# A hybrid encoder step on one core: one band output product for both parts of the probabilities, and four edits beside it

## The chip, the cores and the metric

The kernel is one launch on one core of a Trainium2 chip. The metric is the device time of the launch in microseconds (us). The engines are TensorE (PE, matmuls; PEld is its weight loading), VectorE (DVE), ScalarE (ACT), GpSimd (POOL) and SyncE (SP), which here issues every DMA.

## The reference

One layer of a streaming encoder over 2048 prompt rows and 32 sample rows of width 1024. What matters for the change is the band attention of eight heads of 64 dims, in which each chunk of 64 rows sees itself and the eight chunks before it, the merge, and the MLP with its gate:

```python
def band_core(q, k, v, bias, mask):
    s = jnp.einsum('bqhd,bkhd->bhqk', q, k).astype(jnp.float32) * (HEAD_DIM ** -0.5) + bias[None]
    s = jnp.where(mask, s, NEG)
    p = jax.nn.softmax(s, axis=-1)
    return jnp.einsum('bhqk,bkhd->bqhd', p.astype(v.dtype), v)

def merge(oa, ob, subln_g, out_norm_b, w_out, lam_init):
    ...
    return jnp.concatenate([oa.reshape(B, T, WIDTH_A), ob], axis=-1) @ w_out

def ffn_ple(h, p, g_mlp, w_up, w_down, w_ple_gate, w_ple_proj):
    c = rmsnorm(h, g_mlp)
    h = h + jnp.square(jax.nn.relu(c @ w_up)) @ w_down
    return h + jax.nn.sigmoid(h @ w_ple_gate) * (p @ w_ple_proj)
```

All inputs are 32-bit. Before these, one projection makes queries, keys and values of a differential attention (group A, four heads) and of the band attention (group B); y is normalized at the end, and new keys and values are outputs too.

## The kernel before

**Numbers in two parts.** A 32-bit number is split (`split`, L177) into a high part, rounded to the matmul's format, and a low part, the rest. A product is three matmuls, high by high, high by low, low by high (`mm3`, L211; its lines L215, L216, L217 stand in the profile for every product made that way, told apart by the name of the output: qps and vps for the projections, ops for the output projection, ups and dps for the MLP's up and down products, gps and pps for the gate). The split's copy runs on ScalarE (L180) or VectorE (L182), its subtraction on GpSimd (L165, L175, cut into pieces of 256 columns) or VectorE (L186).

**Stages.** Tokens are in four blocks of 512 (the last with the 32 sample rows, 544). The program, `run`, goes through: norm and values of blocks 0 and 1; projections and group A attention of the first half (to about 515 us); band attention `attn_b` for four groups of query blocks, among projections, output projection and the first MLP chunks (515 to 1216); group A attention of the second half with the MLP of blocks 0 and 1 (to 2110); gate and final norm of block 1; output projections of blocks 2 and 3, `outproj`, with the loading of the second's input, `oload`, woven in, one unit (`OW` = 1) per step (2160 to 2270); gate of block 0 with `cparts(2)`, the operands of block 2's MLP (to 2327); `mlp7(2)`; gate of block 2 with `cparts(3)`; `mlp7(3)`; gate and final norm of block 3.

**What sets the order.** The code is written as generators that `weave` steps alternately. The framework then schedules with its own timeline model, keeping each engine's program order where priorities say so; so instructions of `attn_b` stand among those of the stages written around it. Every buffer belongs to a tag of a pool with a number of copies, and a tile waits for the last user of the copy that it takes. Every load and store (`dma`, L156) is issued by SP, in order: one that waits holds all behind it.

**Band attention.** `attn_b` loads, per head and query group, keys (kbt), queries and values. `attn_b_pair` takes 256 queries, two tiles of 128 with up to five key tiles each. For each tile: scores in one or two banks, two matmuls each (sb, L802); bias and maximum (L805); exponentials (L810) and the division (L812); transposes of the probabilities (tpb, L817); their high part on ScalarE (pHb, L826) and low part on VectorE (pLb, L827). Behind both tiles stands the output product (ob, L842): the value tile (vbt), which holds 64 high and 64 low columns, is the weight; the high and the low probabilities are two matmuls into the same 256 columns (or 128, for a key tile that only one query tile sees). Rows 0 to 63 of ob are then the high values' part and 64 to 127 the low values' part, which L846 and L847 add.

**Values.** `vtile` makes one 128-row tile of values (vps), scales it (vraw, L421) and splits it into vhl: the copy on VectorE, the subtraction on GpSimd.

**mlp7.** 16 chunks of 256 hidden columns. A chunk's up product uses seven block products in place of eight: from the weight's four quarters a11, a12, a21, a22 it makes a11, a12 and five sums s2, s1, s3, s4, a22, each split into pieces (`piece`). The first product needs a11, the second a12, the third s2. The chunk's down products (dps) are added to h (L1124), which is 2 MB and loaded by `hload` before. ReLU and square make u, split into uh and ul (L1138). Down products of a chunk are stepped among the up products of the next one.

Of the kernel before, what the change touches and what calls it, by code (L numbers as in the profile page):

```python
# [12 lines left out]
F32 = mybir.dt.float32  # L13
# [129 lines left out]
class Kern:  # L143
# [261 lines left out]
    def vtile(self, b, i, grp, c, u, acts, sg, mm):  # L405
# [18 lines left out]
        self.split(hl[:n, :, 0], hl[:n, :, 1], r3[:n], "dve", "pool")  # L424
# [165 lines left out]
    def attn_a_pair(self, g, j, kt, ba, pool, ps_s, ps_t, ps_o):  # L590
# [88 lines left out]
        o = ps_o.tile([P, 256], F32, tag="o", name="o")  # L679
# [48 lines left out]
        ss = ps_o.tile([P, 256], F32, tag="o", name="ss")[:, :nq]  # L728
# [6 lines left out]
    def attn_b(self, js, pool, ps_s, ps_t, ps_o):  # L735
# [3 lines left out]
        ke = KC if last else 256 * (js[-1] + 1)  # L739
        for h in range(8):  # L740
# [21 lines left out]
            for x, j in enumerate(js):  # L762
                nq = 256 if j < 8 else SS
                self.attn_b_pair(
                    h, j if j < 8 else None, kt, v, kb, bb, qs[x], tt[:, 256 * x : 256 * x + nq], pool, ps_s, ps_t, ps_o
                )
# [3 lines left out]
    def attn_b_pair(self, h, j, kt, v, kb, bb, q, t1, pool, ps_s, ps_t, ps_o):  # L770
# [7 lines left out]
        pH = pool.tile([P, 6, 256], F32R, tag="pH", bufs=2, name="pHb")  # L778
        pL = pool.tile([P, 6, 256], F32R, tag="pL", bufs=2, name="pLb")
        spans = []  # L780
        for qi, t in enumerate(tiles):
# [14 lines left out]
            e = pool.tile([P, 640], F32, tag="e", bufs=4, name="eb")[:nr, :n]  # L796
            st = pool.tile([P, 5], F32, tag="st", bufs=4, name="stb")[:nr]
            for i in range(nb):
                s = ps_s.tile([P, 512], F32, tag="s", name="sb")[:nr, :w]
                for hl in range(2):  # L800
                    c = k0 - kb + w * i
                    nc.tensor.matmul(  # L802
                        s, q[:, hl, P * qi : P * qi + nr], kt[:, c : c + w], start=hl == 0, stop=hl == 1
                    )
                nc.vector.tensor_tensor_reduce(  # L805
                    e[:, w * i : w * i + w], s, bb[:nr, b0 + w * i : b0 + w * i + w], 1.0, -3e38,
                    ALU.add, ALU.max, st[:, 3 + i : 4 + i],
                )
            nc.vector.tensor_reduce(st[:, 0:1], st[:, 3 : 3 + nb], axis=AX.X, op=ALU.max, negate=True)
            nc.scalar.activation(e, e, AF.Exp, bias=st[:, 0:1], accum_out=st[:, 1:2])  # L810
            nc.vector.reciprocal(st[:, 2:3], st[:, 1:2])
            nc.scalar.activation(e, e, AF.Copy, scale=st[:, 2:3])  # L812
            for x0 in range(0, len(kts), 4):
                ch = kts[x0 : x0 + 4]
                tp = ps_t.tile([P, 4, P], F32, tag="tp", name="tpb")
                for x, (i, kn) in enumerate(ch):
                    nc.tensor.transpose(  # L817
                        tp[:kn, x, :nr], e[:, P * (x0 + x) : P * (x0 + x) + kn], self.ident[:nr, :nr]
                    )
                groups = [(0, len(ch), P)] if not samp else [(0, 1, P), (1, 1, SS)]  # L820
                for a0, na, kn in groups:
                    sl = ch[0][0] - kfirst + a0
                    h_ = pH[:kn, sl : sl + na, P * qi : P * qi + nr]
                    l_ = pL[:kn, sl : sl + na, P * qi : P * qi + nr]
                    s_ = tp[:kn, a0 : a0 + na, :nr]
                    nc.scalar.activation(h_, s_, AF.Copy)  # L826
                    nc.vector.tensor_tensor(l_, s_, h_.bitcast(F32), op=ALU.subtract)  # L827
        o = ps_o.tile([P, 256], F32, tag="o", name="ob")
        order = []
# [9 lines left out]
        for x, (i, kn, qa, qb) in enumerate(order):  # L839
            vt = v[:kn, (SP - kb) // P + i] if samp else v[:kn, i - kb // P]  # L840
            for y, pt in enumerate((pH, pL)):
                nc.tensor.matmul(  # L842
                    o[:, qa:qb], vt, pt[:kn, i - kfirst, qa:qb],
                    start=x == 0 and y == 0, stop=x == len(order) - 1 and y == 1,
                )
        nc.scalar.activation(t1, o[64:128, :nq], AF.Copy)  # L846
        nc.vector.tensor_tensor(t1, o[0:64, :nq], t1, op=ALU.add)  # L847
# [248 lines left out]
    def mlp7(self, b, h, ops, wk, up, mm, md):  # L1096
# [49 lines left out]
        prev = iter(())  # L1146
        for ch in range(DFF // (2 * P)):
# [9 lines left out]
            w = {}  # L1157
            for x in ("a11", "a12", "s2", "s1", "s3", "s4", "a22"):
                w[x] = self.piece([4, P])
# [7 lines left out]
            for x, t, e in (("s2", s2, "dve"), ("s1", a11, "pool"), ("s3", a21, "dve"), ("s4", a12, "pool"), ("a22", a22, "dve")):  # L1167
                self.split(*w[x], t, "act", e)
            us = []
# [155 lines left out]
    def run(self):  # L1325
        tc, nc, a = self.tc, self.nc, self.a
        with ExitStack() as top:
# [24 lines left out]
            with ExitStack() as x:  # L1352
# [7 lines left out]
                def first():  # L1360
                    self.consts(cp)
# [129 lines left out]
            hh = opened(top, "hh", 2, side="right")  # L1491
# [17 lines left out]
            for _ in range(2):  # L1509
                next(m)  # L1510
# [7 lines left out]
            for _ in range(2):  # L1518
                next(m)
# [52 lines left out]
```

## Time and profile before

| | us |
|---|---|
| time, median of 3 runs | 3192.19 (3191.18 to 3198.04) |
| the profiled execution's own time | 3198.91 |
| its span | 3197.1 |
| TensorE, band attention's window | 515 to 1216 |
| mlp7(2): first up product | 2327.13 |

A row of a timeline gives start, duration, engine, line, operation, tiles, shape and count. A row of waits says which engine stood idle before which group, what it waited for, how long in total, how many times, and the longest. A row of groups gives shape and count, busy time and mean ns of one, and the idle time before them. A matmul's duration runs past the start of the next.

### The profile page before, as it was taken

How to read it: one execution, taken by the hardware profiler on the slowest of the kernel's cores; microseconds unless marked ns; L12 is line 12 of the kernel's file. 1: busy time of each engine (PE TensorE's matmuls, PEld its weight loads, DVE VectorE, ACT ScalarE, POOL GpSimd, SP SyncE). 2: the span in 40 equal slices, each digit the busy share in tenths (PEclk: the TensorE clock that was granted, in tenths of full speed). 3: DMA queues.
4: the chain of work that ended last, by engine and by line, in shares of the span. 5: the costliest groups of instructions: out<-in, count | busy, mean ns of one | idle time of the engine just before them, and what ended most of it. 6: DMA issues, size and time to landing. Idle time of an engine off the chain costs nothing.

```text
span 3197.1 us, 53415 instructions
## 1 busy us (share of the span) xinstructions
PE 3033.6 (95%) x18265; PEld 2684.4 (84%) x18265; DVE 1843.7 (58%) x4448; ACT 1884.9 (59%) x4166; POOL 1890.6 (59%) x2572
## 2 busy tenths in 40 slices
PE   8999898899999998999999999998999999899998
PEld 7787787899987787877788888777888888899998
DVE  5147774444464554766756665435577665776663
ACT  5257775766675765666666666444555555554445
POOL 4357455343335544565655555577887778867674
PEclk9999998999999999999999999999999999999999
DMA  8788757886788746555564543537524334233231
GB/s 274 237 244 232 210 182 230 245 228 201 204 238 238 212 120 148 153 154 151 158 184 123 142 126 104 156 109 225 172 87 147 106 100 128 92 100 107 93 114 55
DMA packets 512504, 521.61 MB, mean 163 GB/s; under 512 B 37948, under 2 KB 393600, under 8 KB 512232
## 3 DMA queue, kind: packets, MB, share of 16 engines
q1 hardware_dynamic: 512232, 518.19, 55.4%
q8 instruction: 145, 2.38, 0.3%
q14 instruction: 127, 1.04, 0.1%
HBM read 412.08 MB, written 109.95 MB: 163 GB/s over the span
## 4 chain that ended last, share of the span: by engine, by line
PE 65%; DVE 11%; DMA 10%; ACT 5%; POOL 4%; issue 4%; SPq 1%; DVEq 0%; POOLq 0%; ACTq 0%
PE dps L215 6%; PE dps L217 6%; PE dps L216 6%; PE ups L215 6%; PE ups L216 5%; PE ups L217 5%; PE qps L215 3%; PE qps L216 3%; PE qps L217 3%; PE s L632 3%; DMA oraw<-oT 2%; PE ob L842 2%; PE sb L802 1%; DMA wr<-w_up 1%; PE tpb L817 1%
## 5 line engine op out<-in xcount | busy, mean ns | idle before, releaser
L175 POOL TENSOR_TENSOR wl<-wr,wh 128x256 fp32r<-128x256 f32 x648 | 479.5, 773 | 344.4 <-ACT wh L180 311.5
L180 ACT ACTIVATE piece<-wr 128x512 fp32r<-128x512 f32 x412 | 252.7, 626 | 288.5 <-PE ups L216 139.2
L175 POOL TENSOR_TENSOR piece<-wr,piece 128x256 fp32r<-128x256 f32 x416 | 338.7, 840 | 103.9 <-ACT piece L180 85.2
L180 ACT ACTIVATE wh<-wr 128x1024 fp32r<-128x1024 f32 x228 | 240.7, 1056 | 180.3 <-PE qps L216 46.6
L165 POOL TENSOR_TENSOR wl<-wr,wh 128x256 fp32r<-128x256 f32 x264 | 196.3, 775 | 171.3 <-ACT wh L180 171.1
L215 PE MATMUL ups<-cs,piece 128*128 128x256 f32 (+1 forms) x896 | 257.0, 287 | 10.2 <-ACT piece L180 7.6
L217 PE MATMUL ups<-cs,piece 128*128 128x256 f32 (+1 forms) x896 | 257.1, 287 | 5.6 <-POOL piece L175 5.6
L216 PE MATMUL ups<-cs,piece 128*128 128x256 f32 (+1 forms) x896 | 256.1, 286 | 0.5 <-DVE cs L186 0.5
L216 PE MATMUL dps<-ul,piece 128*128 128x272 f32 (+1 forms) x768 | 247.7, 324 | 1.6 <-DVE ul L186 1.6
L217 PE MATMUL dps<-uh,piece 128*128 128x272 f32 (+1 forms) x768 | 247.5, 324 | 1.3 <-POOL piece L165 1.3
L215 PE MATMUL dps<-uh,piece 128*128 128x272 f32 (+1 forms) x768 | 246.4, 324 | 1.5 <-DVE h L1124 0.8
L165 POOL TENSOR_TENSOR piece<-wr,piece 128x256 fp32r<-128x256 f32 x280 | 224.3, 833 | 25.7 <-ACT piece L180 24.3
L1124 DVE TENSOR_TENSOR h<-h,dps 128x272 f32<-128x272 f32 (+1 forms) x384 | 190.6, 514 | 81.4 <-PE dps L217 80.4
L215 PE MATMUL qps<-aH,wh 128*128 128x512 f32 (+1 forms) x640 | 230.8, 361 | 6.9 <-DVE ql L475 4.8
L1083 DVE TENSOR_TENSOR h<-h,dps 128x512 f32<-128x512 f32 x256 | 174.2, 682 | 96.3 <-PE dps L217 94.7
L217 PE MATMUL qps<-aH,wl 128*128 128x512 f32 (+1 forms) x640 | 229.2, 358 | 0.0
L216 PE MATMUL qps<-aL,wh 128*128 128x512 f32 (+1 forms) x640 | 228.9, 358 | 0.0
L215 PE MATMUL dps<-uh,wh 128*128 128x512 f32 x512 | 211.3, 413 | 13.7 <-DVE h L1083 8.6
L632 PE MATMUL s<-ka,q 128*128 128x512 f32 (+3 forms) x768 | 187.6, 343 | 25.4 <-ACT e L646 17.5
L215 PE MATMUL ups<-cH,wh 128*128 128x512 f32 x512 | 203.6, 398 | 1.6 <-DVE h L1083 0.9
L638 DVE TENSOR_REDUCE nm<-s 128x1 f32<-128x512 f32 (+3 forms) x256 | 147.2, 587 | 98.9 <-PE s L632 97.9
L217 PE MATMUL dps<-uh,wl 128*128 128x512 f32 x512 | 204.0, 398 | 0.0
(298 smaller groups left out, 9793.3 us busy)
## 6 DMA issues: line engine op xcount, KB each, us to landing
wr<-w_up SPq DMA_DIRECT2D x128, 512.0 KB, 4.0
wr<-w_down SPq DMA_DIRECT2D x128, 512.0 KB, 3.7
wr<-w_in SPq DMA_DIRECT2D x74, 512.0 KB, 5.1
q<-qS SPq DMA_DIRECT2D x128, 256.0 KB, 5.4
v<-vSa SPq DMA_DIRECT2D x64, 512.0 KB, 4.3
ka<-kS SPq DMA_DIRECT2D x32, 512.0 KB, 9.0
wr<-w_out SPq DMA_DIRECT2D x32, 512.0 KB, 5.2
wr<-w_ple_gate SPq DMA_DIRECT2D x32, 512.0 KB, 3.9
```

Source lines behind the costliest of these rows:

```text
L165: nc.gpsimd.tensor_tensor(out[:, sl], a[:, sl], b[:, sl], op=op)
L175: nc.gpsimd.tensor_tensor(out[:, sl], a[:, sl], b[:, sl], op=op)
L180: nc.scalar.activation(hi, raw, AF.Copy)
L215: nc.tensor.matmul(ps, lh, rh, start=start and i == 0, stop=False)
L216: nc.tensor.matmul(ps, lh, rl, start=False, stop=False)
L217: nc.tensor.matmul(ps, ll, rh, start=False, stop=stop and i == n - 1)
L632: nc.tensor.matmul(s, q[:, m, hl, P * qi : P * qi + nr], kt[:, m, k0 - kb : k0 - kb + n], start=hl == 0, stop=hl == 1)
L638: nc.vector.tensor_reduce(nmx, s, axis=AX.X, op=ALU.max, negate=True)
L802: nc.tensor.matmul(s, q[:, hl, P * qi : P * qi + nr], kt[:, c : c + w], start=hl == 0, stop=hl == 1)
L842: nc.tensor.matmul(o[:, qa:qb], vt, pt[:kn, i - kfirst, qa:qb], start=x == 0 and y == 0, stop=x == len(order) - 1 and y == 1,)
L1083: nc.vector.tensor_tensor(hv, hv, ps, op=ALU.add)
L1124: nc.vector.tensor_tensor(hv, hv, ps, op=ALU.add)
```

## The change

Five edits.

1. The output product of the band moves to `attn_b_out`: high and low probabilities lie side by side in one tile pb, [128, 6, 2, 256], and each key tile is one matmul over both, 512 columns (or two times 128). The two halves of ob are 256 columns each, of a full bank; a further addition on VectorE adds the low probabilities' part. The product of the low values with the low probabilities, which was in the sum, is left out of it.
2. In the band, `step` and `late` write a tile's transposes (and, with the pair's second tile, the output product and a head's store) behind the next tile's scores.
3. `oload(3)` is stepped by two units for each step of `outproj(2)`.
4. `mlp7` makes chunk 0's first four pieces (a11, a12, s2, s1) in its first step, which `along` puts into the gate before it, once `cparts` is done. They lie in a buffer of the size of h ("lead"), taken from the pool hh, which becomes two pools of one buffer. The rest of chunk 0's pieces are made in the next step. h of the block (`box`) takes the lead's buffer, so its load waits for the last product that reads the lead.
5. `vtile`'s subtraction goes from GpSimd to VectorE.

```diff
@@ vtile
-        self.split(hl[:n, :, 0], hl[:n, :, 1], r3[:n], "dve", "pool")
+        self.split(hl[:n, :, 0], hl[:n, :, 1], r3[:n], "dve", "dve")
@@ attn_b
+        late = []
+
+        def step(first):
+            ins = first()
+            if late:
+                with self.tc.issue_after(ins):
+                    late.pop(0)()
+
...
-            self.dma(self.oT[64 * m : 64 * m + 64, gi, t0 : t0 + n], tt[:, :n])
...
+            late.append(self.then(late.pop(), lambda m=m, gi=gi, tt=tt, t0=t0, n=n: self.dma(
+                self.oT[64 * m : 64 * m + 64, gi, t0 : t0 + n], tt[:, :n]
+            )))
+        late.pop(0)()
@@ attn_b_pair
-        pH = pool.tile([P, 6, 256], F32R, tag="pH", bufs=2, name="pHb")
-        pL = pool.tile([P, 6, 256], F32R, tag="pL", bufs=2, name="pLb")
...
+            def first(qi=qi, nr=nr, k0=k0, n=n, b0=b0, nb=nb, w=w, held=held):
...
+                return ins.ins
+
+            def second(qi=qi, nr=nr, kts=kts, held=held, end=t is tiles[-1]):
+                if qi == 0:
+                    px.append(pool.tile([P, 6, 2, 256], F32R, tag="p", bufs=2, name="pb"))
+                p = px[0]
...
+                        h_, l_ = (p[:kn, sl : sl + na, i, P * qi : P * qi + nr] for i in range(2))
...
+                if end:
+                    self.attn_b_out(samp, nq, spans, kfirst, kb, v, px[0], t1, ps_o)
+
+            step(first)
+            late.append(second)
+
+    def attn_b_out(self, samp, nq, spans, kfirst, kb, v, p, t1, ps_o):
+        nc = self.nc
+        o = ps_o.tile([P, 512], F32, tag="o", name="ob").rearrange("p (i c) -> p i c", i=2)
...
-            for y, pt in enumerate((pH, pL)):
-                nc.tensor.matmul(
-                    o[:, qa:qb], vt, pt[:kn, i - kfirst, qa:qb],
-                    start=x == 0 and y == 0, stop=x == len(order) - 1 and y == 1,
-                )
-        nc.scalar.activation(t1, o[64:128, :nq], AF.Copy)
-        nc.vector.tensor_tensor(t1, o[0:64, :nq], t1, op=ALU.add)
+            nc.tensor.matmul(
+                o[:, :, qa:qb], vt, p[:kn, i - kfirst, :, qa:qb], start=x == 0, stop=x == len(order) - 1
+            )
+        nc.scalar.activation(t1, o[64:128, 0, :nq], AF.Copy)
+        nc.vector.tensor_tensor(t1, o[0:64, 0, :nq], t1, op=ALU.add)
+        nc.vector.tensor_tensor(t1, o[0:64, 1, :nq], t1, op=ALU.add)
@@ mlp7
+    def along(self, c, m):
+        for _ in c:
+            yield
+        yield
+        next(m)
+        yield
...
+        def weights(ch, w, piece):
...
+            self.split(*w["s2"], s2, "act", "dve")
+            self.split(*w["s1"], a11, "act", "pool")
+            yield
+            for x in ("s3", "s4", "a22"):
+                w[x] = self.piece([4, P])
+            for x, t, e in (("s3", a21, "dve"), ("s4", a12, "pool"), ("a22", a22, "dve")):
                 self.split(*w[x], t, "act", e)
+
+        w = {}
+        lead = hh.tile([P, 8, BLK], F32R, tag="h", name="lead").rearrange("p k c -> p (k c)")
+        leads = iter(lead[:, 512 * i : 512 * i + 512].rearrange("p (k c) -> p k c", c=P) for i in range(8))
+        g = weights(0, w, lambda shape: [next(leads), next(leads)])
+        next(g)
+        yield
+        drain(g)
+        h = hh.tile([P, 8, BLK], F32, tag="h", name="h")
+        self.dma(h[:, :, :n], self.hS[:, :, 512 * b : 512 * b + n])
+        box.append(h)
@@ run
-            hh = opened(top, "hh", 2, side="right")
+            hh = [opened(top, f"hh{i}", 1, side="right") for i in range(2)]
...
-                weave(self.outproj(2, wk, oa[2], md, acc[2]), self.oload(3, wk, act, oa), 1, 0, OW)
+                weave(self.outproj(2, wk, oa[2], md, acc[2]), self.oload(3, wk, act, oa), 1, 0, 2)
...
-            weave(g, self.cparts(2, wk, cs, ops, r2), 1)
+            c = self.cparts(2, wk, cs, ops, r2)
+            next(c)
+            box = []
+            m = self.mlp7(2, hh[1], box, ops[2], wk, up, mm, md)
+            weave(g, self.along(c, m), 1)
             f = self.final(0, h, up, fk, mm)
-            h = hload(hh, BLK, 2)
-            m = self.mlp7(2, h, ops[2], wk, up, mm, md)
             for _ in range(2):
                 next(m)
+            h = box[0]
             weave(m, f, 1)
```

The same is done for block 3, whose lead lies in hh[0].

On PE, at a full pair of the band, before (ob is the output product, tpb the transposes):

```order
L842 MATMUL ob<-pLb,vbt 128x256
L842 MATMUL ob<-pHb,vbt 128x256
L842 MATMUL ob<-pLb,vbt 128x256
L842 MATMUL ob<-pHb,vbt 128x256
L842 MATMUL ob<-pLb,vbt 128x256
L842 MATMUL ob<-pHb,vbt 128x256
L842 MATMUL ob<-pLb,vbt 128x256
L842 MATMUL ob<-pHb,vbt 128x128
L842 MATMUL ob<-pLb,vbt 128x128
L842 MATMUL ob<-pHb,vbt 128x128
L842 MATMUL ob<-pLb,vbt 128x128
L817 MATMUL tpb<-ident,eb 128x128 x5
```

and after, with the scores (sb) of the tile ahead and pieces of a value projection (vps):

```order
L824 MATMUL sb<-kbt,q 128x320 x2
L217 MATMUL vps<-wh,aL 128x256
L215 MATMUL vps<-wh,aH 128x256
L216 MATMUL vps<-wl,aH 128x256
L876 MATMUL ob<-pb,vbt 128x512 x4
L876 MATMUL ob<-pb,vbt 128x2x128 x2
L846 MATMUL tpb<-ident,eb 128x128 x5
```

Twelve matmuls (the first stands a few rows ahead, before a projection's) became six, and the next tile's scores and a projection stand before them.

On SP, whose rows are the DMAs in their order (h of block 2, and wr for every raw weight), at the end of the second output projection, before:

```order
L156 DMA hd_25587<-xT_76 128x544
L156 DMA hd_25670<-xT_76 128x544
L156 DMA h_26788<-hS_82 128x8x512
L156 DMA wr_26205<-w_ple_proj 128x2x512
L156 DMA hS_82<-hd_25587 128x544
L156 DMA hS_82<-hd_25670 128x544
```

and at mlp7(2)'s beginning, before, where each pair of w_up rows is a chunk:

```order
L156 DMA wr_26952<-w_up 128x4x256
L156 DMA wr_27041<-w_down 128x2x512
L156 DMA wr_27135<-w_down 128x2x512
L156 DMA wr_27198<-w_up 128x4x256
L156 DMA wr_27200<-w_up 128x4x256
```

The same beginning after; the four w_up rows are chunk 1's and chunk 2's two halves (chunk 0's stand far ahead, in the gate):

```order
L156 DMA wr_26594<-w_up 128x4x256
L156 DMA wr_26685<-w_down 128x2x512
L156 DMA wr_26596<-w_up 128x4x256
L156 DMA wr_26779<-w_down 128x2x512
L156 DMA wr_26842<-w_up 128x4x256
L156 DMA h_26473<-hS_82 128x8x512
L156 DMA wr_26844<-w_up 128x4x256
L156 DMA wr_26933<-w_down 128x2x512
L156 DMA wr_27027<-w_down 128x2x512
```

The load of h, 2 MB, went from ahead of the gate to between the two halves of chunk 2.

On DVE, in chunk 1 of mlp7(2), before (u2, u3, r0, r1 are block products, ul the low part of a chunk's u, s2 and wr the weight sums of chunk 2, h the sum with the down products):

```order
L1135 TENSOR_TENSOR r1_26836<-u3_26896,ups_26931 128x256
L1163 TENSOR_TENSOR wr_27198<-wr_27198 128x4x128
L186 TENSOR_TENSOR ul_26832<-r0_26835,uh_26831 128x512
L1135 TENSOR_TENSOR r0_26995<-t1_26997,ups_27012 128x256
L1164 TENSOR_TENSOR s2_27222<-wr_27200,wr_27198 128x512
L1135 TENSOR_TENSOR u2_27026<-t1_26997,ups_27027 128x256
L1135 TENSOR_TENSOR u3_27084<-u2_27026,ups_27085 128x256
L1165 TENSOR_TENSOR wr_27198<-s2_27222,wr_27198 128x4x128
L1124 TENSOR_TENSOR h_26788<-h_26788,dps_27053 128x512
```

and after:

```order
L1176 TENSOR_TENSOR r0_26479<-u2_26510,ups_26557 128x256
L1176 TENSOR_TENSOR r0_26639<-t1_26641,ups_26656 128x256
L1176 TENSOR_TENSOR u2_26670<-t1_26641,ups_26671 128x256
L1204 TENSOR_TENSOR s2_26860<-wr_26844,wr_26842 128x512
L186 TENSOR_TENSOR ul_26476<-r0_26479,uh_26475 128x512
L186 TENSOR_TENSOR piece_26851<-s2_26860,piece_26850 128x512
L1205 TENSOR_TENSOR wr_26842<-s2_26860,wr_26842 128x4x128
L1176 TENSOR_TENSOR u3_26728<-u2_26670,ups_26729 128x256
L1176 TENSOR_TENSOR r0_26639<-u2_26670,ups_26761 128x256
L1165 TENSOR_TENSOR h_26473<-h_26473,dps_26697 128x512
```

Chunk 0's ul stood ahead of the operation that takes both halves of chunk 2 (L1164, now L1204) and now stands behind it.

More of the change, by code (lines that the diff above doesn't have):

```diff
@@ L809, in attn_b_pair @@
[L809 to L827, printed above, removed]
@@ L828, in attn_b_pair @@
-        o = ps_o.tile([P, 256], F32, tag="o", name="ob")
-        order = []
+            held = []
+            def first(qi=qi, nr=nr, k0=k0, n=n, b0=b0, nb=nb, w=w, held=held):
+                e = pool.tile([P, 640], F32, tag="e", bufs=4, name="eb")[:nr, :n]
+                st = pool.tile([P, 5], F32, tag="st", bufs=4, name="stb")[:nr]
+                held.append(e)
+                for i in range(nb):
+                    s = ps_s.tile([P, 512], F32, tag="s", name="sb")[:nr, :w]
+                    for hl in range(2):
+                        c = k0 - kb + w * i
+                        ins = nc.tensor.matmul(
+                            s, q[:, hl, P * qi : P * qi + nr], kt[:, c : c + w], start=hl == 0, stop=hl == 1
+                        )
+                    nc.vector.tensor_tensor_reduce(
+                        e[:, w * i : w * i + w], s, bb[:nr, b0 + w * i : b0 + w * i + w], 1.0, -3e38,
+                        ALU.add, ALU.max, st[:, 3 + i : 4 + i],
+                    )
+                nc.vector.tensor_reduce(st[:, 0:1], st[:, 3 : 3 + nb], axis=AX.X, op=ALU.max, negate=True)
+                nc.scalar.activation(e, e, AF.Exp, bias=st[:, 0:1], accum_out=st[:, 1:2])
+                nc.vector.reciprocal(st[:, 2:3], st[:, 1:2])
+                nc.scalar.activation(e, e, AF.Copy, scale=st[:, 2:3])
+                return ins.ins
@@ new lines, in second @@
+            def second(qi=qi, nr=nr, kts=kts, held=held, end=t is tiles[-1]):
+                if qi == 0:
+                    px.append(pool.tile([P, 6, 2, 256], F32R, tag="p", bufs=2, name="pb"))
+                p = px[0]
+                e = held[0]
+                for x0 in range(0, len(kts), 4):
+                    ch = kts[x0 : x0 + 4]
+                    tp = ps_t.tile([P, 4, P], F32, tag="tp", name="tpb")
+                    for x, (i, kn) in enumerate(ch):
+                        nc.tensor.transpose(
+                            tp[:kn, x, :nr], e[:, P * (x0 + x) : P * (x0 + x) + kn], self.ident[:nr, :nr]
+                        )
+                    groups = [(0, len(ch), P)] if not samp else [(0, 1, P), (1, 1, SS)]
+                    for a0, na, kn in groups:
+                        sl = ch[0][0] - kfirst + a0
+                        h_, l_ = (p[:kn, sl : sl + na, i, P * qi : P * qi + nr] for i in range(2))
+                        s_ = tp[:kn, a0 : a0 + na, :nr]
+                        nc.scalar.activation(h_, s_, AF.Copy)
+                        nc.vector.tensor_tensor(l_, s_, h_.bitcast(F32), op=ALU.subtract)
+                if end:
+                    self.attn_b_out(samp, nq, spans, kfirst, kb, v, px[0], t1, ps_o)
@@ L1513, in run @@
             next(g)
[L1514 removed]
+            c = self.cparts(3, wk, cs, ops, r3)
+            next(c)
+            box = []
+            m = self.mlp7(3, hh[0], box, ops[3], wk, up, mm, md)
+            weave(g, self.along(c, m), 1)
             f = self.final(2, h, up, fk, mm)
[L1516 to L1517 removed]
             for _ in range(2):
                 next(m)
+            h = box[0]
             weave(m, f, 1)
```

49 lines of the change are left out of this document (22 added, 27 removed).

## The prediction

> **What bounds the kernel now.** I read the page first, for which engine carries the end, then the stretch that the largest edit touches, then the waits of the places that the other edits aim at. The page:
>
> ```profile
> span 3197.1 us, 53415 instructions
> PE 3033.6 (95%) x18265; PEld 2684.4 (84%) x18265; DVE 1843.7 (58%) x4448; ACT 1884.9 (59%) x4166; POOL 1890.6 (59%) x2572
> PE 65%; DVE 11%; DMA 10%; ACT 5%; POOL 4%; issue 4%; SPq 1%; DVEq 0%; POOLq 0%; ACTq 0%
> ```
>
> TensorE (PE) is busy 95% of the span and has 65% of the chain that ended last; every other engine is under 60%. So time comes off where PE's instructions get fewer or shorter, or where PE stands waiting; other engines' work counts only when PE waits for it. The window from 515 to 1216 us holds the band attention, interleaved with projections, output products and the first MLP chunks (columns: window, length, busy time of PE, PEld, DVE, ACT, POOL, granted clock, DMA share, GB/s):
>
> ```profile
> 515.00:1216.00 701.00, 670.45 (x4359) 603.37 (x4358) 350.16 (x1233) 465.98 (x982) 305.93 (x472) 0.99 0.73 208
> ```
>
> PE is busy 670 of 701 us there, VectorE (DVE) 350. What PE is spared in this window shortens it almost one for one, and VectorE has half its time free.
>
> **A, the band's output product.** A matmul's duration overlaps its neighbours', so its price is the distance from its start to the next one's. PE's timeline gives it, 512 columns first, then 256, then 128:
>
> ```profile
> 839.82 0.40 PE L217 MATMUL qps<-aH,wl 128*128 128x512 f32 x1
> 840.52 0.40 PE L217 MATMUL qps<-aH,wl 128*128 128x512 f32 x1
> 861.46 0.28 PE L842 MATMUL ob<-pLb,vbt 128*128 128x256 f32 x1
> 862.17 0.28 PE L842 MATMUL ob<-pLb,vbt 128*128 128x256 f32 x1
> 862.28 0.22 PE L842 MATMUL ob<-pHb,vbt 128*128 128x128 f32 x1
> 862.34 0.28 PE L842 MATMUL ob<-pLb,vbt 128*128 128x128 f32 x1
> 862.68 0.51 PE L817 MATMUL tpb<-ident,eb 128*128 128x128 f32 x3
> ```
>
> The first two are three matmuls apart: 0.70/3 = 0.233 us for 512 columns. The next two are six apart: 0.71/6 = 0.118 for 256. From 862.34 to the transposes at 862.68 are three: 0.34/3 = 0.113 for 128, hardly less than for 256, so a matmul of 128 columns is held up by something other than its columns. The counts:
>
> ```profile
> L842 PE MATMUL ob<-pHb,vbt 128*128 128x256 f32 x224 | 59.7, 287 | 1.0 <-ACT pHb L826 1.0
> L842 PE MATMUL ob<-pLb,vbt 128*128 128x128 f32 x112 | 29.6, 277 | 0.0
> ```
>
> With as many of the other part, that is 448 of 256 columns and 224 of 128. The change makes 224 of 512 and 112 of two times 128, which I price as one of 256. Of the 224, 192 are in 48 full query pairs (8 heads, j = 2 to 7). Such a pair had 8 of 256 and 4 of 128; the eleven of one pair that the timeline shows in a row take 862.68 - 861.46 = 1.22, and the twelfth 0.118: 1.34. After, 4 × 0.233 + 2 × 0.118 = 1.17. That is 0.17 × 48 = 8.2 us less. The two short pairs of each head lose one or three double matmuls of 256 and one of 128: 2 × 0.118 + 2 × 0.113 against 0.233 + 0.118 is 0.11 each (the 256s cancel), 16 × 0.11 = 1.8. The eight sample pairs go from four matmuls of 32 columns to two, at about 0.11 each: 1.8. Sum 11.8, so **A = -12**. Were a matmul of two times 128 as dear as two of 128, 0.226, the 112 of them would cost 12 us more and A would be 0: the near bound. With 8 × 0.118 + 4 × 0.113 = 1.40 for a pair before, it saves 0.23, and A is -15: the far bound. The rows of 256 and 512 columns both follow the column count, so I stay near them.
>
> The Trainium skill, page "TensorE: Matmul & The Clock Gate", section "Back-to-back issue gap", gives an isolated matmul N/2.4 + 2.5 ns: 56, 109 and 216 ns. By it a pair would fall from 8 × 109 + 4 × 56 = 1096 ns to 4 × 216 + 2 × 109 = 1082, and A would be under -1. The same section calls the formula too low at small N, which the 0.113 above bears out.
>
> **B, the band's lag by one tile.** In the order before, a tile's transposes follow its own scores with other work between; after, the next tile's scores stand between as well. The waits of PE in the window (what waits, what for, total, times, longest):
>
> ```profile
> PE sb L802 <- DVE stb L805: 6.5, 10, 1.5
> PE ob L842 <- ACT pHb L826: 2.5, 4, 1.5
> PE tpb L817 <- DVE pLb L827: 1.9, 3, 1.2
> ```
>
> These sum to 10.9, and a lag can only take such waits. The first is a wait for a free score bank, which a lag does not remove by itself; the others, 4.4, it should. I take **B = -5**, between -11 and +6, the latter if as many new waits come at score banks as there are now. A head's store of its output goes out one tile later on SP; nothing in the band reads it.
>
> **C, two units of oload(3) for each step of outproj(2).** PE's waits from 2190 to 2240:
>
> ```profile
> PE ops L215 <- ACT oact L180: 6.5, 2, 4.8
> ```
>
> Unit after unit, oload's split was the last to come. With two units a step the last of them stands four steps earlier, so the 6.5 should go. Its loads stand ahead of outproj's weights on SP by as much, and those take
>
> ```profile
> wr<-w_out SPq DMA_DIRECT2D x32, 512.0 KB, 5.2
> ```
>
> to land, against 24 × 0.233 = 5.6 us of products in a step: little to spare. **C = -6**, between -6.5 and 0, where a weight is as late as the split was.
>
> **D, chunk 0's weights of mlp7 made inside the gate.** PE's waits at the two transitions into mlp7, first from 2315 to 2345, then from 2725 to 2756:
>
> ```profile
> PE ups L215 <- ACT piece L180: 4.0, 1, 4.0
> PE ups L217 <- POOL piece L175: 2.7, 1, 2.7
> ...
> PE ups L215 <- ACT piece L180: 3.6, 1, 3.6
> PE ups L217 <- POOL piece L175: 3.0, 1, 3.0
> ```
>
> That is 13.3. Each is dearer than its idle time, since PE comes back at half pace:
>
> ```profile
> 2339.46 0.41 PE L215 MATMUL ups<-cs,piece 128*128 128x256 f32 x1
> 2339.67 0.41 PE L216 MATMUL ups<-cs,piece 128*128 128x256 f32 x1
> ```
>
> 0.21 apart where 0.118 is usual, for an estimated 1 to 2 us more at each transition. So up to 14 could go. But h of the block now has to wait for the lead buffer, and its load stands in SP's queue between the two halves of chunk 2's up weights (the second order fence, with the change). What such a load takes, from the place where before made one of 2 MB, and what a weight issued 2.3 us behind it took:
>
> ```profile
> h<-hS SPq DMA_DIRECT2D x1, 2048.0 KB, 10.7
> wr<-w_out SPq DMA_DIRECT2D x1, 512.0 KB, 10.1
> ```
>
> Chunk 2's first half was issued late before:
>
> ```profile
> 2327.13 0.28 PE L215 MATMUL ups<-cs,piece 128*128 128x256 f32 x1
> 2347.16 0.37 SPq L156 DMA_DIRECT2D wr<-w_up  x1
> ```
>
> 20 us after the first product of mlp7, of which some 8.5 were the stall (4.0 + 2.7 and the slow stretch): 11.5 without it. The h load goes out right behind it, and chunk 2's second half then lands, by the two rows above, some 18 to 24 us after the first product. On VectorE the operation that needs that half (L1204) now stands ahead of chunk 0's u split (the third order fence). PE wants that split when chunk 0's seven products and three of chunk 1 are through, 10 × 12 × 0.118 = 14 us after the first: a new wait of some 4 to 10 us at the first transition. At the second the split stands ahead of it and only h can be late:
>
> ```profile
> L1124 DVE TENSOR_TENSOR h<-h,dps x16: 671/674/689, 2361.3 to 2392.2; 128x512 f32<-128x512 f32 x16
> ```
>
> The first addition to h came 34 us after the first product, 25 without the stall, so a load issued 12 after it and 11 long is in time. The bounds: -14, where all of it goes and nothing comes; +8, where the waits are only moved into the gates, whose VectorE now makes these sums and splits beside the sigmoids, and the second half is 8 late on top. No row shows a gate with this work in it, so I take the middle, **D = -3**.
>
> **E, the values' second part and the third addition on VectorE.** The operations as they are, POOL's split, VectorE's like it, and the addition:
>
> ```profile
> L175 POOL TENSOR_TENSOR vhl<-vraw,vhl x68: 723/738/924, 17.3 to 787.4; 128x256 fp32r<-128x256 f32 x64, 32x256 fp32r<-32x256 f32 x4
> L186 DVE TENSOR_TENSOR cs<-tmp,cs x40: 407/956/978, 2290.1 to 2742.7; 128x256 fp32r<-128x256 f32 x20, 128x272 fp32r<-128x272 f32 x20
> L847 DVE TENSOR_TENSOR t<-ob,t x72: 169/414/418, 534.3 to 1214.4; 64x256 f32<-64x256 f32 x64, 64x32 f32<-64x32 f32 x8
> ```
>
> 68 splits at 0.41 to 0.96 and 72 additions at 0.414, so 30 us of additions and 28 to 65 of splits, on an engine with 350 us free in the band window; what hides them is PE's 670 us there. POOL loses 50 us. **E = 0**, between -5 (a tenth of POOL's 50 comes back as weight splits that are sooner) and +8 (a twelfth of 30 + 65 reaches PE).
>
> The Trainium skill, page "SBUF — State Buffer", section "SBUF: two separate sides", says that a VectorE operation with two SBUF inputs and a GpSimd operation that reads SBUF lock each other out for a whole instruction. The spread from 407 to 956 ns above agrees; by it each of the 68 could cost 0.41 + 0.74 = 1.15, 78 us in all, still within VectorE's free time.
>
> **Sum:** -12 - 5 - 6 - 3 + 0 = -26 from the profiled execution's own 3198.9 us (span 3197.1 and 1.8 around it): 3172.9. The median of the runs before is 6.7 below that execution, so I forecast **3166**.
>
> **The rivals.**
> 1. Late weights behind h: D becomes +8 at both transitions. For it: the queue order and the 10.1 us landing. Against: at the second transition the split is ahead. 3166 + 11 = 3177.
> 2. The band saves nothing: the time that PE is spared is given back as waits at score banks (the 6.5 above grows by what A and B save), since scores, exponentials and splits keep their pace. For it: VectorE's wait of the scores is on the path in ten places already. Against: PE is 96% busy there and interleaved with work that does not wait for the band. Only C and D: 3192 - 9 = 3183. That the change does not do what it says would give the same; the order shows that it does.
> 3. Columns alone set PE's pace: a matmul of 128 columns costs 0.059, half of 0.118, and a pair before 8 × 0.118 + 4 × 0.059 = 1.18, as after. A is -1 and the time 3177. For it: one such step, 862.28 to 862.34. Against: the three that follow at 0.113.
> 4. Slower: VectorE's added operations, 30 us of additions and 50 of splits, are in the chain from a score bank to its release, in the band window. Break-even is where 26 of the 80 reach PE, a third; at half, +14 and 3206. For it: that engine has 11% of the chain. Against: its 50% in the window.
>
> **How the numbers follow.** Forecast 0.62 (3150 to 3182: A to E at half of their bounds); rival 1 0.15; rival 2 0.10; rival 3 0.03; rival 4 0.06; the rest, no effect at all, 0.04. The range must hold 0.8: the forecast's own, rivals 1 and 3, and most of rival 2; below, all terms at their far bounds, 15 + 11 + 6.5 + 14 + 5 = 51.5, would give 3141, and I stop a little short of that. So **3144 to 3190**. 0.2% (6.4 us) is about what a measurement of this kernel can tell from no change. Faster by more: forecast, rivals 1 and 3 and half of 2, 0.85. Same: 0.09. Slower: rival 4, 0.06.
>
> **What would show it.** A: the band's matmuls 0.233 and 0.118 apart, and PE's busy time in the window down by about 12 while its idle time (30.5) does not grow. B: the waits of tpb and ob gone, sb's no larger. C: no ops wait over 1 us from 2190 to 2240. D: the four waits for piece gone, and at the first transition a new one of PE for ul, ended by VectorE behind the second half's load. E: VectorE's splits of vhl near 0.41 to 0.96 with no PE wait that ends on them. I am wrong if PE's idle time in the window grows by over 10, if the gates before mlp7 become longer by what the transitions lose, or if the 2 x 128 form costs over 0.2.

## The result and the profile after

| | before | changed |
|---|---|---|
| median of four runs each, us | 3195.11 (3191.18 to 3203.04) | 3168.34 (3161.89 to 3174.89) |
| ratio | | 0.9919, 95% interval 0.9901 to 0.9938 |
| profiled execution's own time, us | 3198.91 | 3174.89 |

The kernel became 26.8 us faster by the medians; 26 were forecast. The terms that make up the sum came out otherwise, though. The page of the changed kernel, its first lines:

```profile
span 3173.1 us, 52702 instructions
PE 3023.9 (95%) x17913; PEld 2664.6 (84%) x17913; DVE 1900.0 (60%) x4588; ACT 1880.8 (59%) x4166; POOL 1835.6 (58%) x2504
```

TensorE has 352 instructions and 9.7 us less, VectorE 56 us more, GpSimd 55 less. To see where time went I cut both spans at places of the program: the first score of the band, the first product of gate(1), of outproj(2) and of gate(0), and the last down product of mlp7(3). The windows between them, of before (columns as in the prediction):

```profile
518.83:2102.26 1583.43, 1519.49 (x8623) 1313.52 (x8621) 884.47 (x2397) 1011.02 (x2219) 810.18 (x1173) 0.99 0.61 174
2163.82:2270.82 107.00, 100.08 (x599) 89.69 (x600) 49.07 (x78) 45.62 (x96) 85.47 (x110) 0.97 0.78 241
2270.82:3118.30 847.48, 826.31 (x5542) 765.85 (x5540) 584.10 (x1009) 448.26 (x846) 643.25 (x782) 0.99 0.35 108
```

and of the changed kernel:

```profile
519.41:2077.99 1558.58, 1504.40 (x8272) 1290.44 (x8271) 924.64 (x2497) 1007.59 (x2220) 786.37 (x1143) 0.99 0.62 177
2138.73:2242.20 103.47, 97.95 (x599) 88.22 (x600) 50.11 (x79) 46.24 (x96) 84.63 (x109) 0.98 0.74 230
2242.20:3094.28 852.08, 829.68 (x5541) 768.89 (x5540) 585.49 (x1007) 449.42 (x846) 637.93 (x783) 0.99 0.35 110
```

From the first score to gate(1), which I call the middle: 24.9 us shorter, of which PE's busy time is 15.1 and its idle time 9.8 (63.9 to 54.2). The output projections: 3.5 shorter. From gate(0) to mlp7's end: 4.6 longer. The rest of the span is within 1 us.

The fixed window that the prediction names for A, 515 to 1216 us, reads after the change:

```profile
515.00:1216.00 701.00, 676.61 (x4090) 595.43 (x4089) 391.65 (x1338) 469.72 (x990) 301.99 (x461) 0.99 0.74 211
```

PE's busy time in it rose by 6, from 670.45, where the prediction had it fall by about 12; its idle time fell from 30.5 to 24.4. The sign could not come true: in a window of fixed length PE's busy time can fall only if its idle time grows, which the prediction excluded. The middle, which begins and ends at the same instructions, shows the fall.

**The output product.** A full pair on PE's timeline of the changed kernel:

```profile
843.15 1.32 PE L876 MATMUL ob<-pb,vbt 128*128 128x512 f32 x6
844.31 0.49 PE L846 MATMUL tpb<-ident,eb 128*128 128x128 f32 x3
```

Six matmuls take 844.31 - 843.15 = 1.16 us; 1.17 was worked out, against 1.34 before.

**The seam.** The wait that shrank most in the middle stands at the seam, where the band ends and the second half's group A attention begins (its scores are `s`, L632). In brackets stand the idle time and what ended it; first the longest wait there before, then the one in the changed kernel:

```profile
1247.69 0.80 PE L632 MATMUL s<-ka,q 128*128 128x512 f32 x1 [8.05 <-ACT e L646]
```

```profile
1227.48 0.72 PE L632 MATMUL s<-ka,q 128*128 128x512 f32 x2 [2.03 <-DMA q<-qS]
```

Before, the scores wait 8.05 us there for an exponential (e, L646) that frees their bank. In the changed kernel no score waits for an exponential there; the first of them wait 2.03 us for a load. The orders of the two programs at this place, as runs of matmuls on PE:

```
before:  s 6, ups 14, dps 6, s 6, dps 12, s 6, dps 12, s 4, dps 12, s 2, tpp 4, ...
changed: s 6, ups 23, s 2, ups 1, s 2, ups 1, s 2, ups 20, s 6, ups 3, dps 6, tpp 4, ...
```

No edit is written at this place; the scheduler, working from its model of time, put more of the MLP's up products there: 25 among the first twelve scores, where before had 14. The middle gave some of this back. Further on, group A's output product (o) waits for ScalarE, which it did not do before:

```profile
PE o L718 <- ACT pH L711: 7.4, 3, 3.8
```

**Output projections.** The wait of ops for oact is gone. A new one has come behind outproj(2):

```profile
2198.66 0.52 PE L1044 MATMUL css<-sh,ones_r 128*128 128x512 f32 x1 [4.86 <-ACT sh L180]
```

It is the sum of squares for block 2's norm. ScalarE makes its input, behind the last addition of that projection (hd), a square and GpSimd's sum:

```profile
2195.77 0.63 ACT L974 ACTIVATE tmp<-hd 128x512 f32<-128x512 f32 x1 [3.21 <-DVE hd L969]
...
2197.98 0.63 ACT L180 ACTIVATE sh<-sqacc 128x512 fp32r<-128x512 f32 x1 [1.58 <-POOL sqacc L165]
```

**mlp7.** The four waits for piece are gone. PE's waits of the changed kernel in 2285 to 2335:

```profile
PE gps L215 <- DVE sig L1300: 4.7, 1, 4.7
PE dps L215 <- ACT uh L180: 3.8, 1, 3.8
PE ups L215 <- DVE r L1176: 1.5, 1, 1.5
```

and in 2700 to 2745:

```profile
PE gps L215 <- DVE sig L1300: 4.5, 1, 4.5
PE ups L215 <- DVE r L1176: 2.4, 1, 2.4
PE dps L215 <- ACT uh L180: 1.1, 1, 1.1
```

That is 18.0 us of new waits against 13.3 that went. From a gate's first product to the first row of mlp7's products it was 56.3 and 56.4 us before and is 64.5 and 63.5 now, 15.3 more in all; from there to mlp7's end it is 3.0 and 7.6 less. The first group is the gate's: L1300 frees a bank of the gate's product, and it stands behind a row of cparts' and the weights' operations without a gap:

```profile
2293.87 1.21 DVE L186 TENSOR_TENSOR piece<-wr,piece 128x512 fp32r<-128x512 f32 x1
...
2297.40 0.68 DVE L1300 SCALAR_TENSOR_TENSOR sig<-gps,sig 128x512 f32<-128x512 f32 x1
```

The second group begins with a load. SP and VectorE:

```profile
2316.47 0.37 SPq L156 DMA_DIRECT2D wr<-w_up  x1
2316.93 0.55 SPq L156 DMA_DIRECT2D h<-hS  x1
```

```profile
2320.40 0.69 DVE L1203 TENSOR_TENSOR wr<-wr 128x512 f32<-128x512 f32 x1 [3.22 <-DMA wr<-w_up]
```

VectorE stands 3.22 us before L1203, the first operation on chunk 2's weights, whose first half was issued only at 2316.47; chunk 0's products (r, L1176) are queued behind it. It is the first half that is late, ahead of h, and not the second half behind h. At the second transition VectorE stands 3.14 us at the same place.

### The profile page after: what moved, and what is told of

It is laid out like the page before. It is cut to its first block, busy times and chain, and to the rows that moved or that the text cites. A ratio compares the mean times of both kernels' runs of the same rounds, so it can differ in the third digit from the quotient of the medians.

```text
span 3173.1 us, 52702 instructions
## 1 busy us (share of the span) xinstructions
PE 3023.9 (95%) x17913; PEld 2664.6 (84%) x17913; DVE 1900.0 (60%) x4588; ACT 1880.8 (59%) x4166; POOL 1835.6 (58%) x2504
## 3 DMA queue, kind: packets, MB, share of 16 engines
q1 hardware_dynamic: 512232, 518.19, 55.4%
## 5 line engine op out<-in xcount | busy, mean ns | idle before, releaser
L175 POOL TENSOR_TENSOR piece<-wr,piece 128x256 fp32r<-128x256 f32 x404 | 325.3, 831 | 101.8 <-ACT piece L180 88.7
L215 PE MATMUL ups<-cs,piece 128*128 128x256 f32 (+1 forms) x864 | 248.2, 288 | 5.0 <-DVE r L1176 5.0
L217 PE MATMUL ups<-cs,piece 128*128 128x256 f32 (+1 forms) x864 | 247.9, 287 | 0.0
L216 PE MATMUL ups<-cs,piece 128*128 128x256 f32 (+1 forms) x864 | 247.5, 287 | 0.0
L165 POOL TENSOR_TENSOR piece<-wr,piece 128x256 fp32r<-128x256 f32 x280 | 223.6, 830 | 27.1 <-ACT piece L180 25.2
L632 PE MATMUL s<-ka,q 128*128 128x512 f32 (+3 forms) x768 | 187.6, 345 | 17.7 <-ACT e L646 7.2
L216 PE MATMUL dps<-ul,wh 128*128 128x512 f32 x512 | 202.3, 395 | 0.0
```

Of the source, the lines that this page charges most:

```text
L165: nc.gpsimd.tensor_tensor(out[:, sl], a[:, sl], b[:, sl], op=op)
L175: nc.gpsimd.tensor_tensor(out[:, sl], a[:, sl], b[:, sl], op=op)
L215: nc.tensor.matmul(ps, lh, rh, start=start and i == 0, stop=False)
L216: nc.tensor.matmul(ps, lh, rl, start=False, stop=False)
L217: nc.tensor.matmul(ps, ll, rh, start=False, stop=stop and i == n - 1)
L632: nc.tensor.matmul(s, q[:, m, hl, P * qi : P * qi + nr], kt[:, m, k0 - kb : k0 - kb + n], start=hl == 0, stop=hl == 1)
```

## The experiments

Each ratio is against runs of before on the same chip. The table has them with the middle, from one profiled execution each (idle is length less PE's busy time), and how many up products stand among the first twelve scores at the seam, read from the program's order. The changed kernel stands first.

| kernel | ratio (95% interval) | middle, us | PE busy | idle | ups at seam |
|---|---|---|---|---|---|
| changed | 0.9919 (0.9901 to 0.9938) | 1558.6 | 1504.4 | 54.2 | 25 |
| no_b | 0.9935 (0.9923 to 0.9947) | 1558.6 | 1506.8 | 51.8 | 25 |
| no_c | 0.9945 (0.9929 to 0.9960) | 1555.6 | 1504.9 | 50.7 | 25 |
| no_d | 0.9917 (0.9903 to 0.9932) | 1551.5 | 1504.5 | 47.1 | 25 |
| d_raw | 0.9919 (0.9906 to 0.9933) | 1555.3 | 1503.9 | 51.4 | 25 |
| d_rawl | 0.9908 (0.9895 to 0.9921) | 1552.2 | 1503.9 | 48.4 | 25 |
| e_b | 0.9946 (0.9931 to 0.9962) | 1556.7 | 1505.8 | 51.0 | 25 |
| e_1 | 0.9964 (0.9952 to 0.9976) | 1555.1 | 1503.2 | 51.9 | 25 |
| e_h1 | 0.9987 (0.9977 to 0.9997) | 1566.3 | 1505.3 | 61.0 | 0 |
| no_de | 0.9983 (0.9972 to 0.9993) | 1573.0 | 1510.2 | 62.8 | 0 |
| no_e | 1.0006 (0.9995 to 1.0016) | 1566.0 | 1506.9 | 59.1 | 0 |
| a_two | 1.0018 (1.0007 to 1.0030) | 1577.0 | 1519.9 | 57.1 | 0 |
| no_a | 1.0018 (1.0007 to 1.0029) | 1579.6 | 1519.4 | 60.2 | 0 |
| before | | 1583.4 | 1519.5 | 63.9 | 14 |

**no_a**, the output product undone:

```diff
-            nc.tensor.matmul(
-                o[:, :, qa:qb], vt, p[:kn, i - kfirst, :, qa:qb], start=x == 0, stop=x == len(order) - 1
-            )
+            for y in range(2):
+                nc.tensor.matmul(
+                    o[:, qa:qb], vt, p[:kn, i - kfirst, y, qa:qb],
+                    start=x == 0 and y == 0, stop=x == len(order) - 1 and y == 1,
+                )
...
-        nc.vector.tensor_tensor(t1, o[0:64, 1, :nq], t1, op=ALU.add)
```

> The changed kernel with the band's output product as it was: two matmuls for each key tile, high and low probabilities one after the other into the same 256 columns, and without the third addition; the lag, oload's pace, mlp7 and the values' split stay as changed. If the saved matmuls are what the band gained, it is 12 us slower than the changed kernel, about 3180, and PE's busy time between 515 and 1216 us is up by 12. If the gain up to gate(1) (24 us in the two traces) comes from the order that the scheduler chose, it is within 4 us of the changed kernel, and the gate of block 1 begins near 2078 us as in the changed kernel.

In the window from 515 to 1216 PE's busy time reads 673.1 against 676.6 in the changed kernel, so the expected rise of 12 isn't there; over the middle, which holds the same work in both, it rose by 13 to 15. But the loss was 0.8% or some 27 us against no_b, twice the 12, and gate(1) began at 2095 and not near 2078. Both theories miss the size: the matmuls are half of it, and the idle time is back at 60.

**no_b**, the lag undone: `step` only calls `first()`, and `second()` is called right behind it.

> The changed kernel without the lag: a tile's transposes are written behind its own scores again. If the lag takes PE's waits in the band, it is 5 to 12 us slower than the changed kernel (3173 to 3180), and the waits of ob and tpb for ScalarE and VectorE are back at 4 us or more. If the lag does nothing, it is within 3 us of the changed kernel.

Nothing, and for a plain reason: the two programs have the same instructions in the same order on all five engines. The scheduler puts the transposes where they were written without the lag too. So no_b is a second measurement of the changed kernel, and the two tell how far a single profiled execution scatters: the first score comes at 519.4 in one and 515.0 in the other, the last stretch is 852.1 and 849.8 long, the middle the same.

**no_c**, `oload(3)` by one unit:

```diff
-weave(self.outproj(2, wk, oa[2], md, acc[2]), self.oload(3, wk, act, oa), 1, 0, 2)
+weave(self.outproj(2, wk, oa[2], md, acc[2]), self.oload(3, wk, act, oa), 1, 0, OW)
```

> The changed kernel with one unit of oload(3) for each step of outproj(2). By the wait that went (6.5 us in the trace of before, 2.3 left after) the stretch from the first product of outproj(2) to the gate of block 0 is 3 to 6 us longer than the 103.3 of the changed kernel, and the time 3171 to 3175; if a weight is late in the split's place anyway, the stretch stays within 1 us.

The stretch is 106.8 against 103.5 (102.8 in no_b): 3.3 to 4.0 us, as expected, and the whole time, 3 us above no_b, agrees within its interval. The waits from 2127.7 to 2234.6 show what C trades:

```profile
PE ops L215 <- ACT oact L180: 5.6, 3, 5.2
PE ops L215 <- ACT piece L180: 1.8, 1, 1.8
PE css L1044 <- ACT sh L180: 0.5, 1, 0.5
```

With C the 5.6 for oact goes and the 0.5 for css becomes 4.9. In no_e, which has C, it becomes 7.0 and the stretch is 107.0: no gain at all. With C the stretch is 102.8 to 104.5 in the kernels with 25 up products at the seam and 104.0 to 107.0 in those with none, so what C gains hangs on the order too.

**no_d**, mlp7 and the loads of h as before (the diff's part of `mlp7` and `run` undone, but for oload's pace).

> The changed kernel with mlp7 and the loads of h as they were: all of chunk 0's weights made in mlp7's first step, h loaded ahead of the gate. If the prediction's term holds (a gain of 3), it is 3 us slower than the changed kernel, 3171. If the two traces are read rightly, in which the stretch from the gate of block 0 to the last down product of mlp7(3) went from 847.5 to 852.1 us, it is 4 to 5 us faster, 3164, and that stretch is 847 to 848 long again.

The stretch from gate(0) to mlp7's end is 847.3, as expected from the traces. It is 847.5 in before, 844.5 in no_de, and 849.8 to 853.8 in the nine kernels that have the edit as it was made. The whole time is 0.0018 of before's below no_b, with intervals that overlap; no_de against no_e, 0.0023, has ones that don't.

**no_e**, the values' subtraction on GpSimd, and **no_de**, both undone.

> The changed kernel with the values' subtraction on GpSimd again. Bookkeeping over the runs so far (0.9930 for the changed kernel, whose program no_b turned out to be, 1.0018 without the output product, gains of C and a loss of D between) leaves a loss of about 4 us for this edit: then the ratio is about 0.9917. If the edit costs nothing, as the prediction had it, the ratio is 0.9930.

> The changed kernel with mlp7 and the loads of h as before, and the values' subtraction on GpSimd. If the losses of both edits are real and add up (4 us each), the ratio is about 0.9904; if only mlp7's is, 0.9917; if neither is more than noise, 0.993.

Both expectations fell, and the bookkeeping that they came from with them. The edit that I had put at nothing is worth 0.0071 or 23 us beside the output product, and the output product without it little (no_de 0.9983, with C). The two do not add: without either one, the time is within 0.2% of before's. In the middle PE's busy time stays at 1507 us in no_e; it is the idle time that is 5 to 12 longer than in the kernels with both, and the wait at the seam is back.:

```profile
1228.01 0.79 PE L632 MATMUL s<-ka,q 128*128 128x512 f32 x1 [7.21 <-ACT e L646]
```

Of the 23 us the traces place 5 to 7 in this idle time (59.1 against the 54.2 and 51.8 of the changed kernel's two profiles) and some 4 in the output projections.

**a_two**, the new tiles and bank with two matmuls for each key tile:

```diff
-        for x, (i, kn, qa, qb) in enumerate(order):
...
-            nc.tensor.matmul(
-                o[:, :, qa:qb], vt, p[:kn, i - kfirst, :, qa:qb], start=x == 0, stop=x == len(order) - 1
-            )
+        for y in range(2):
+            for x, (i, kn, qa, qb) in enumerate(order):
...
+                nc.tensor.matmul(
+                    o[:, y, qa:qb], vt, p[:kn, i - kfirst, y, qa:qb], start=x == 0, stop=x == len(order) - 1
+                )
```

> The changed kernel, with its tile of high and low probabilities side by side, its full bank of two halves and its third addition, but with two matmuls for each key tile, one for each half. If what the edit gains (some 27 us by no_a, of which the matmuls' own steps explain 14) comes from the number of matmuls alone, this run is about as slow as no_a, a ratio of 1.002. If half of it comes from the new bank layout or the order that goes with it, the ratio is about 0.9975.

As slow as no_a: layout and third addition bring nothing by themselves. It has the other order at the seam, too.

**d_raw**, chunk 0's raw weights in the lead, its pieces in the ring:

```diff
-                raws.append(self.rawp.tile([P, 4, 256], F32, bufs=2, name="wr"))
+                raws.append(spare[i] if ch == 0 else self.rawp.tile([P, 4, 256], F32, bufs=2, name="wr"))
...
-        g = weights(0, w, lambda shape: [next(leads), next(leads)])
+        spare = [lead[:, 1024 * i : 1024 * i + 1024].rearrange("p (k c) -> p k c", c=256) for i in range(2)]
+        g = weights(0, w, self.piece)
```

> The changed kernel with chunk 0's raw up weights in the lead buffer in place of its four pieces, which go through the usual ring: so the ring of raw weights is not held by chunk 0, and chunk 2's loads can be issued earlier; h waits only for the raw weights. If the new waits in mlp7 (1.5 + 3.8 and 2.4 + 1.1 us in the trace after) come from chunk 2's load, issued late for want of a buffer, they go, and the stretch from the gate of block 0 to the last down product of mlp7(3) is 843 us against the 852 after; the waits of gps for VectorE stay. If they come from VectorE's load in general, the stretch stays at 850 to 852.

Of the new waits in mlp7, 8.8 us in all, 1.8 are left (uh at the first transition), and the stretch is 845.8, some 5 shorter than with the edit as made. But chunk 2's load is not issued sooner:

```profile
2309.71 1.77 SPq L156 DMA_DIRECT2D wr<-w_up  x2
```

Its first half goes out 76.6 us after the gate's first product, against 74.3 with the edit as made. What comes sooner is chunk 1: its two halves go out 31.9 and 36.4 us after the gate's first product, against 47.0 and 59.3. PE makes chunk 0's first products among the gate's last ones, from 55.4 us on, and on VectorE the first operation on chunk 2 (L1203) now stands behind chunk 0's products. So the waits went with another order, in which VectorE does not stand before chunk 2's weights while chunk 0's products are due; that a raw buffer kept by chunk 0 was what held back chunk 2's load is not shown. The gates' waits stay, for VectorE 2.7 at the first and at the second

```profile
PE gps L215 <- DVE sig L1300: 6.5, 1, 6.5
```

**d_rawl**, d_raw with one more `yield` in `along` ahead of the weights.

> d_raw with chunk 0's early weights one gate step later, behind more of cparts' work on VectorE. If the waits of gps for VectorE in the gates (2.7 and 6.5 us in d_raw) come from the weight sums standing among cparts' operations, they shrink below 2 each and the stretch from the gate of block 0 to the last down product of mlp7(3) falls from 845.8 to about 839, the time to a ratio of 0.990. If VectorE's row is too long in the gate in any order, or the first products come late instead, the stretch stays within 3 us of 845.8.

The waits in the gates change places (2.5, 1.9, then 4.6, 1.7, 1.6), and the stretch is 845.8 again: moving the work by a step does not help. This is the fastest kernel that was run, though its interval touches those of the changed kernel and of no_d; that it beats them is not shown.

**e_b**, the subtraction on VectorE for the band's values alone (34 of 68 operations), **e_h1**, for blocks 0 and 1 alone (32), **e_1**, for block 1 alone (16). They part two theories. The scheduler's order at the seam is that of the changed kernel in e_b and e_1 and that of no_e in e_h1, whatever the number of operations. The lines for e_b:

```diff
-        self.split(hl[:n, :, 0], hl[:n, :, 1], r3[:n], "dve", "dve")
+        self.split(hl[:n, :, 0], hl[:n, :, 1], r3[:n], "dve", "dve" if grp == 1 else "pool")
```

e_h1 has `b < 2` in place of `grp == 1`, and e_1 `b == 1`.

> The changed kernel, in which only the band values' subtraction (34 of the 68 operations) is on VectorE; group A's is on GpSimd. The scheduler's order at the seam from the band to the second half's group A attention is that of the changed kernel: up products (ups) stand among the first scores there. Theory 1, that the output product and the values' split gain together because of the order that they lead the scheduler to: as fast as the changed kernel, a ratio of 0.993. Theory 2, that GpSimd's relief or VectorE's load does it, operation by operation: half way between 1.0006 (no_e) and 0.993, so 0.997.

> The changed kernel, in which the values' subtraction is on VectorE for blocks 0 and 1 and on GpSimd for blocks 2 and 3: half of the operations again. The scheduler's order at the seam is that of no_e: down products alone stand among the first scores, and the up products come later. Theory 1 (the order): as slow as no_e, a ratio of 1.000 with the wait of s for ACT e of some 7 us at the seam. Theory 2 (operation by operation): 0.997.

> The changed kernel, in which the values' subtraction is on VectorE for block 1 alone, 16 of the 68 operations, all of which are among the 32 of e_h1. Yet the scheduler's order at the seam is that of the changed kernel again. Theory 1 (the order): a ratio near 0.993, well below e_h1's 0.9987, though half of e_h1's operations have gone back to GpSimd. Theory 2 (operation by operation): 0.999.

e_b and e_h1 have as many operations moved, and differ by 0.0041, 13 us, with intervals apart: operation by operation they would be alike. e_1 is faster than e_h1 with half of its operations, which speaks the same way, though from another chip and with intervals that only just part, and its wait at the seam is short:

```profile
1228.27 0.96 PE L632 MATMUL s<-ka,q 128*128 128x512 f32 x3 [2.27 <-DMA q<-qS]
```

In the middle the order parts the kernels cleanly: idle is 47.1 to 54.2 in the eight with 25 up products at the seam, 57.1 to 62.8 in the five with none, and 63.9 in before, with 14. The programs bear this out beyond the seam: from 1069 us of the changed kernel on, PE's order to the end of the middle is one and the same in all eight, and no_e, no_de and e_h1 share another from the middle's first product to its last. One and the same order reads from 47.1 to 54.2 (changed, no_b, no_c, no_d, d_raw, d_rawl) or from 59.1 to 62.8 of idle time, so a single trace tells it only to some 7 us. No run forces an order with the edits left alone, and which part of it counts, the seam or the rest, is not shown. And e_1's whole time is 0.9964 and not 0.993. Its middle is as short as the others'; in its one trace the first score comes at 519.2 and the last stretch is 853.8 long, and neither is explained.

## Why the prediction was right, and where it was not

The sum was right, 3166 against 3168, but by luck: of its five terms only the first was.

1. **A, -12.** Right, in mechanism and size, as work of PE: a pair takes 1.16 us, and PE's busy time in the middle is 12 to 17 us lower in the kernels with the edit (9 in no_de) than in no_a, a_two and before. Rival 3 (columns alone) falls with it. That A alone makes the kernel faster is not shown: no_e has these 12 us less and is no faster than before.
2. **B, -5.** Nothing. The step that failed is "after, the next tile's scores stand between as well": I read this from the order of the changed kernel, where it is so, and put it down to the lag. The program without the lag has the same order.
3. **C, -6.** It was -3.5. The wait went as said, but what the step names as next in line, a late load, was not what came: the sum of squares behind outproj(2) became the next wait, 4.9 us.
4. **D, -3.** It was a loss of 4 to 5, inside the bounds. The step took a new wait at one transition only, of 4 to 10 us, behind the h load; it came at both, 5.3 and 3.5, and on chunk 2's first half, ahead of h. So rival 1 (late weights behind h) was wrong about the place too. The gates' filling, for which I had no row, was the dearer part: waits of 4.7 and 4.5, and gates longer by 8.2 and 7.1. That is the prediction's own sign of being wrong, gates that become longer by what the transitions lose.
5. **E, 0.** The step counted the operations where they stand, and there it holds: PE's busy time is the same and no wait of PE ends on them. Its bound of -5 failed: beside the output product the edit is worth 23 us by the runs (no_e), because, as far as the runs show, the two together lead the scheduler to another order. In the traces this takes 5 to 7 us of PE's idle time in the middle, 5 of them at the seam (7.21 to 2.03), and some 4 in the output projections. No rival had it.

So the forecast was kept by terms that offset each other: B's 5, C's missing 2.5 and D's 7.6 were made good by 3 more of A and by the 9.8 us of idle time that the middle lost with an order that nobody wrote.

What stays open: against before, no_e's trace is 19.9 us shorter (17.4 in the middle and 6.3 ahead of it, with 4.5 given back in mlp7), yet its runs are no faster. Its profiled execution, 3178.97, was the fastest of its eleven (median 3185.55), and that of before, 3198.91, above its median of 3195.11, so the two traces show some 10 us too much between them; some 11 us are located by no trace. The granted clock may hold a part of them. Its mean over a kernel's runs is 0.9788 to 0.9799 in the five kernels with no up products at the seam, 0.9798 to 0.9824 in the eight with 25, and 0.9812 to 0.9821 in the runs of before beside them. From no_e's 0.9791 to 0.9818 in before is 0.3%; with PE busy for 95% of the span, I estimate that as at most some 8 us. Whether the clock is a cause of the time or only follows PE's waits, no run tells: behind the wait of 4.86 us for css, products of 272 columns start 0.23 us apart for some 3.5 us, and then 0.125.

## What to carry to other kernels

Where a scheduler sets the order, an edit's own cost and the order that it leads to are two terms, and the second can be as large as the first with no wait that the edit is named in. Build the kernel with a small part of the edit more or less and look at whether the order at the big waits changes; and build it with each edit undone, since one that leaves every engine's order as it was has no effect to predict. Work that is made earlier keeps its input buffers longer: ask which later load takes the same buffers.

## What the runs showed of the hardware

One and the same subtraction of the values took VectorE between 404 and 979 ns in the changed kernel, a spread like that of the prediction's row for cs:

```profile
L186 DVE TENSOR_TENSOR vhl<-vraw,vhl x68: 404/425/979, 18.7 to 772.8; 128x256 fp32r<-128x256 f32 x64, 32x256 fp32r<-32x256 f32 x4
```

Half of them took 425 ns or less, where GpSimd had needed 738: the 64 of 256 columns cost VectorE 31 us (64 × 0.484, their mean), near the prediction's lower bound of 28 for all 68 and far from its 65.
